# A hybrid encoder trunk on one core: threads for the operands of w_in, new build-time costs and yields, and a sixth group of columns in the woven stage

## The chip, the core and the metric

The kernel runs on one core of one Trainium2 chip. The metric is the device time of one execution in microseconds, the median over several runs. The core has a matrix engine (TensorE, PE in the profile, with its weight loads listed as PEld), a vector engine (VectorE, DVE), a scalar engine (ScalarE, ACT), GpSimd (POOL), and SyncE (SP), whose queue issues all of this kernel's DMAs. Each engine executes its own instructions in the order in which they stand in its queue and waits on semaphores for the others.

## The reference

Two inputs of 512 tokens and 1024 channels (0 and 1 here) go through two layers with shared weights. Everything is float32.

```
layer 0 (RWKV-7):  xn = rms_norm(x, pre0);  r, k, v, z = lerp_j(xn) @ w_r, w_k, w_v;  xn @ w_z
   two scans, forward and backward, per head of 64 channels:
   S_t = S_{t-1} (diag(decay_t) + a_t b_t^T) + v_t k_t^T ;   y_t = S_t r_t
   y = group_norm(y_fwd + y_bwd) + bonus;   h = (y * silu(z)) @ w_o
   x1 = x + rms_norm(h, post0)
layer 1 (2-D neighbourhood attention, 16 heads, window 8 x 16):
   q, k, v, z = rms_norm(x1, pre1) @ w_in + b_in          # w_in: 1024 x 4096
   o = softmax(q k^T / 8 + bias) v;   y = x1 + rms_norm((o * silu(z)) @ w_o + b_o, post1)
```

## The kernel before

Activations lie with channels on partitions, so one tile is 128 channels by 512 tokens, and an operand of a projection is eight such tiles. To keep float32 accuracy, every operand and every weight is split into a rounded part `hi` and a rest `lo` (one ScalarE copy and one VectorE subtraction each), and a product is a triplet of matmuls, hi*hi, hi*lo and lo*hi. A column is 128 output channels: eight triplets into one PSUM bank. One weight column of 128 x 1024 is loaded and split in two halves of 128 x 512.

The program has three stages.

The prelude makes the norms and the mixed inputs and the columns of z and k of input 0.

The woven stage holds the scan. The scan runs in chunks of 64 tokens: 64 steps (8 chunks for each of 4 groups of head pairs and 2 inputs, both directions at once). For each group of 8 steps, `prep` (two per group) makes the decayed vectors and Gram matrices, and `inverse` inverts 32 x 32 triangular blocks by elimination on VectorE (30 times a multiplication L941 and an addition L942), transposes, and joins the blocks on PE (L970, L972). `step` runs the chain PE (L1106, L1112), ScalarE, PE (L1133), ScalarE, PE (L1153, L1157), VectorE (L1163 to L1173) to the next state. `finish` normalises a group's result. Beside this run the projections in `flow`: `loads` and `splits` of weights, `fetched` and `operands` of the tile operands, `products` (L751 to L753) and `posts`, which evict a column. They go through a fixed list of groups: r, v of input 0; k, r, v and six columns of z of input 1; w_o of input 0; two columns of z; and last the columns of w_in for input 0, made in order of p, four columns (q, k, v, z) for each p. `NPA` says for how many p this happens here. Products of w_in need operands that are made from h, the result of w_o: x1 = h * post0 * rstd + x (L1526, L1529), a scaled hi and lo (L728, L733), and the sum of squares (L1534, L1538) for the second norm, whose factor is applied at the eviction (`qkvz`, L1331). Before, one thread does all of this for one tile after the other.

The order in the woven stage is decided when the program is built. Each of these parts is a Python generator, a `Thread`, which yields the engine on which it goes on, a gate, and a function for the time at which its inputs are there. `weave` keeps a `Clock` with a time for each engine, and picks the thread of lowest rank among those whose time has come; PE work comes last, and products have rank 9, so they are what fills PE. What stands between two yields of a thread is issued in one piece. The clock's costs and latencies (`LAT`, and the lines in `one`) are only the planner's: on the chip every engine follows its queue and its waits. `NACT` operand buffers, `NXR` buffers for loaded tiles, and `NW` for split weights bound how far ahead the threads go.

In the third stage the framework's scheduler sets the order. `rest` makes the columns of w_in for the remaining p, then w_o of input 1, with attention for input 0 spread beside them: `run` advances the attention generator by `POST0` for each triplet of w_in and by `POST` for each one of w_o. A head pair has two half-heads there (scores L1375, transposes L1393, output L1408). Then come the second layer's end for input 0, and w_in, attention and w_o of input 1.

Of the kernel before, what the change touches and what calls it, by code (L numbers as in the profile page):

```python
# [19 lines left out]
P = 128  # L20
# [30 lines left out]
class Clock:  # L51
# [4 lines left out]
    LAT = dict(P=200.0, A=45.0, D=45.0, G=90.0, S=0.0)  # L56
# [55 lines left out]
    def one(self, e, i):  # L112
# [102 lines left out]
class Trunk:  # L215
    NACT, NW, NRAW, NXR, NTMP, WP = 18, 4, 3, 3, 5, 512
    POST0, POST, POST2, POST3, NPA = 0.7, 1.0, 0.15, 0.66, 5
# [18 lines left out]
    NZ1, STOCK, EPS, NEAR = 6, 1, 60.0, 400.0  # L236
    AHEADE = dict(S=3000.0, A=200.0, D=200.0)
# [16 lines left out]
    def name(self, s):  # L254
        self.uid += 1
        return f"{s}_{self.uid}"
# [424 lines left out]
    def flow(self):  # L681
# [4 lines left out]
        name = lambda *xs: [x.tensor.name for x in xs]  # L686
        raw, w, x, todo = {}, {}, {}, {}
# [21 lines left out]
        def fetched():  # L709
            for g, (ready, source, _) in enumerate(self.groups):  # L710
                for k in range(KT if g else 0):
                    yield "S", lambda: ready() and 8 * g + k < min(did["x"] + self.NACT // 2 + self.NXR - 1, 8 * len(self.groups) - 8 + did["x1"] + self.NXR)
                    todo[g, k] = source(k)

        def operands():
            for g in range(1, len(self.groups)):
                for k in range(KT):
                    yield "S", lambda: (g, k) in todo
                    src, before, by, then = todo.pop((g, k))
                    for e, f in before:  # L720
                        yield e, None, lambda c: c.at(name(src))
                        f()
                    yield "A", lambda: 8 * g + k < did["x"] + self.NACT // 2 - (by is not None), lambda c: c.at(name(src))
                    lo, hi = self.pair()
                    if by is None:
                        nc.scalar.copy(hi, src)
                    else:
                        nc.scalar.activation(hi, src, AF.Identity, scale=by)  # L728
                    yield "D"
                    if by is None:  # L730
                        nc.vector.tensor_tensor(lo, src, hi.bitcast(F32), op=ALU.subtract)  # L731
                    else:
                        nc.vector.scalar_tensor_tensor(lo, src, by, hi.bitcast(F32), op0=ALU.mult, op1=ALU.subtract)  # L733
                    x[g, k] = hi, lo
                    for e, f in then:
                        yield e
                        f()
# [1117 lines left out]
```

## Time and profile before

| | us |
|---|---|
| median of 3 runs | 1693.5 (1692.28 to 1696.38) |
| profiled execution, its own time | 1695.69 |
| span of that execution | 1693.9 |
| PE busy | 1542.3 |
| DVE busy | 1243.6 |
| ACT busy | 987.9 |
| mean granted clock of PE | 0.958 |

The busy times are unions of the instructions' times within the span. A matmul's listed time overlaps that of the next, so the rate of PE is read from start to start. The costliest lines are the triplets of the woven stage (L751 to L753, 608 of each) and of the third stage (L406 to L408).

### The profile page before, as it was taken

What the parts mean: (1) busy time and instruction counts of PE and PEld (TensorE: products, weight loads), DVE (VectorE), ACT (ScalarE), POOL (GpSimd) and SP (SyncE); (2) the same over time, 40 slices, a digit from 0 to 9 for tenths busy, and PEclk for the clock granted to TensorE, in tenths of its full rate; (3) what the DMA queues carried; (4) which work ended last, traced back from release to release, by engine and by line L of the source; (5) the groups of instructions that cost most, each with busy time, mean ns of one, the idle gap of its engine ahead of it and who ended that gap; (6) DMA issues with size and microseconds to landing.
All of it is one profiled execution on the core that took longest, in us unless ns stands there. A gap on an engine that the chain in (4) does not pass through costs nothing.

```text
span 1693.9 us, 45876 instructions
## 1 busy us (share of the span) xinstructions
PE 1542.3 (91%) x18624; PEld 1171.7 (69%) x18624; DVE 1243.6 (73%) x2725; ACT 987.9 (58%) x1979; POOL 24.1 (1%) x94
## 2 busy tenths in 40 slices
PE   7989788889998988889978689999999999999998
PEld 6767556666676766666656477777777887777776
DVE  8985679688786886897878988656566686555564
ACT  5443655767665666667576545544567765555562
POOL 0000000000000000000000000000000000000000
PEclk9989989899999999999989799999999999999999
DMA  5435687786686777885667754557555346545553
GB/s 207 162 124 187 201 286 222 209 257 224 196 258 197 233 230 220 273 262 188 210 226 233 225 181 141 158 169 261 177 184 181 113 138 240 188 155 174 168 175 106
DMA packets 240819, 336.23 MB, mean 198 GB/s; under 512 B 53696, under 2 KB 119360, under 8 KB 240608
## 3 DMA queue, kind: packets, MB, share of 16 engines
q1 hardware_dynamic: 240608, 333.31, 61.2%
q8 instruction: 146, 2.39, 0.6%
q14 instruction: 65, 0.53, 0.1%
HBM read 227.71 MB, written 105.51 MB: 197 GB/s over the span
## 4 chain that ended last, share of the span: by engine, by line
PE 59%; DVE 16%; DMA 9%; ACT 9%; issue 5%; SPq 1%; DVEq 0%; ACTq 0%
PE pg L406 6%; PE pg L407 6%; PE pg L408 6%; PE pm L751 5%; PE pm L752 4%; PE pm L753 4%; PE sc L1375 2%; PE pf L1035 2%; PE po L1408 2%; DVE etmp L941 2%; DVE N L942 2%; PE pt L1393 1%; PE zy L1106 1%; DVE wlo L705 1%; PE us L1133 1%
## 5 line engine op out<-in xcount | busy, mean ns | idle before, releaser
L751 PE MATMUL pm<-act,whi 128*128 128x512 f32 x608 | 272.5, 448 | 19.4 <-ACT whi L703 8.9
L753 PE MATMUL pm<-act,wlo 128*128 128x512 f32 x608 | 249.2, 410 | 13.3 <-DVE wlo L705 11.9
L752 PE MATMUL pm<-act,whi 128*128 128x512 f32 x608 | 248.6, 409 | 11.2 <-DVE act L731 8.3
L406 PE MATMUL pg<-act,whi 128*128 128x512 f32 x480 | 199.8, 417 | 0.0
L407 PE MATMUL pg<-act,whi 128*128 128x512 f32 x480 | 190.2, 396 | 0.0
L408 PE MATMUL pg<-act,wlo 128*128 128x512 f32 x480 | 189.8, 396 | 0.0
L355 ACT CAST whi<-raw 128x512 fp32r<-128x512 f32 x156 | 96.4, 619 | 134.8 <-PE pg L407 87.9
L751 PEld LDWEIGHTS pm<-act,whi 128*128 128x128 f32 x608 | 119.2, 196 | 60.5 <-issue 13.3
L753 PEld LDWEIGHTS pm<-act,wlo 128*128 128x128 f32 x608 | 119.3, 196 | 50.0 <-DVE wlo L705 19.4
L356 DVE TENSOR_TENSOR wlo<-raw,whi 128x512 fp32r<-128x512 f32 x156 | 106.7, 686 | 59.8 <-ACT whi L355 49.8
L752 PEld LDWEIGHTS pm<-act,whi 128*128 128x128 f32 x608 | 119.7, 197 | 34.8 <-DVE act L731 11.4
L705 DVE TENSOR_TENSOR wlo<-raw,whi 128x512 fp32r<-128x512 f32 x152 | 103.3, 684 | 46.8 <-ACT whi L703 43.7
L703 ACT CAST whi<-raw 128x512 fp32r<-128x512 f32 x152 | 93.1, 618 | 31.4 <-PE pm L752 13.1
L408 PEld LDWEIGHTS pg<-act,wlo 128*128 128x128 f32 x480 | 90.7, 189 | 19.9 <-issue 0.7
L406 PEld LDWEIGHTS pg<-act,whi 128*128 128x128 f32 x480 | 90.9, 189 | 19.4 <-issue 4.8
L407 PEld LDWEIGHTS pg<-act,whi 128*128 128x128 f32 x480 | 91.0, 190 | 17.2 <-issue 3.0
L942 DVE TENSOR_TENSOR N<-etmp,N 128x30 f32<-128x30 f32 (+14 forms) x240 | 79.7, 332 | 8.2
L941 DVE TENSOR_TENSOR etmp<-N 128x30 f32<-128x30 f32 (+14 forms) x240 | 78.4, 327 | 4.5
L1386 DVE CUSTOM_DVE_ANT_0 sb<-sc,bias 128x256 f32<-128x256 f32 x128 | 50.5, 420 | 39.8 <-PE pt L1393 29.2
L1389 ACT ACTIVATE sb<-sb,mx 128x256 f32<-128x256 f32 x128 | 64.2, 503 | 16.4 <-DVE mx L1388 16.0
L1035 PE MATMUL pf<-cab 64*64 64x128 f32 (+1 forms) x2048 | 69.9, 274 | 3.7 <-issue 3.1
L1145 ACT COPY X<-us 64x256 f32<-64x256 f32 x128 | 46.8, 366 | 33.7 <-PE zy L1013 31.2
(381 smaller groups left out, 3298.3 us busy)
## 6 DMA issues: line engine op xcount, KB each, us to landing
dab<-ab SPq DMA_DIRECT2D x32, 1024.0 KB, 7.3
cab<-dab SPq DMA_DIRECT2D x64, 512.0 KB, 4.3
raw<-in_w_in_dram SPq DMA_DIRECT2D x128, 256.0 KB, 3.4
bias<-in_rpb_dram SPq DMA_DIRECT2D x32, 384.0 KB, 4.1
raw<-in_w_z_dram SPq DMA_DIRECT2D x32, 256.0 KB, 5.3
dz<-tmp SPq DMA_DIRECT2D x32, 256.0 KB, 3.3
raw<-in_w_k_dram SPq DMA_DIRECT2D x32, 256.0 KB, 2.6
dk<-tmp SPq DMA_DIRECT2D x32, 256.0 KB, 3.1
```

The lines of the kernel that those rows point to most:

```text
L355: self.nc.scalar.copy(hi, src)
L356: (eng or self.nc.vector).tensor_tensor(lo, src, hi.bitcast(F32), op=ALU.subtract)
L406: nc.tensor.matmul(ps, hi, x[k][0], start=(k == 0), stop=False)
L407: nc.tensor.matmul(ps, hi, x[k][1], start=False, stop=False)
L408: nc.tensor.matmul(ps, lo, x[k][0], start=False, stop=(k == KT - 1))
L705: nc.vector.tensor_tensor(lo, raw.pop(h), hi.bitcast(F32), op=ALU.subtract)
L751: nc.tensor.matmul(ps, hi[:, at], xh, start=(k == 0), stop=False)
L752: nc.tensor.matmul(ps, hi[:, at], xl, start=False, stop=False)
L753: nc.tensor.matmul(ps, lo[:, at], xh, start=False, stop=(k == KT - 1))
L941: vt.tensor_tensor(tv, N[:, q + 1:, q:q + 1].broadcast_to([P, n, q]), N[:, q:q + 1, :q].broadcast_to([P, n, q]), op=ALU.mult)
L942: vt.tensor_tensor(N[:, q + 1:, :q], tv, N[:, q + 1:, :q], op=ALU.add)
L1035: end = nc.tensor.matmul(st.f[half(a), h, 0, d, g] if st.last else st.f[half(a), h, :, d, g], ab[half(h), d, g, 2 * e[d] + 1 - a], rt if s ...
```

## The change

- The planner's clock gets other numbers. A result counts as available later on PE, ScalarE, VectorE and GpSimd (`LAT`), a ScalarE operation costs 85 + 0.85 n in place of 175 + 0.86 n, a VectorE one 82 + 1.02 n in place of 80 + 1.06 n ns, and a ScalarE or VectorE operation that reads its own engine's result is charged the latency too.
- Yields are added between dependent vector operations: in `inverse` between L941 and L942 and in two other places, in `step` between L1165 and L1166, in `prep` and in `finish`, so that the planner may put other work between them.
- The operands of w_in are made by three threads, `residual` (x1), `scaled` (hi and lo) and `squares` (the norm's sum), each of rank 0.6 in place of 2.5. A gate lets five sources be under way; two of the eight (`HACT`, tiles 3 and 4) are loaded into operand buffers in place of the three `xr` buffers, and `held` counts the operand buffers in use.
- `NPA` goes from 5 to 6: the columns of w_in for six p are in the woven stage, 80 columns in place of 76, and for two in the third stage in place of three. `POST0` goes from 0.7 to 0.9.

```diff
-    LAT = dict(P=200.0, A=45.0, D=45.0, G=90.0, S=0.0)
+    LAT = dict(P=210.0, A=125.0, D=116.0, G=120.0, S=0.0)
...
-                    if f != e or e == "S":
+                    if f != e or e == "S" or e in "AD" and table is self.made:
...
-                c = 175.0 + 0.86 * n
+                c = 85.0 + 0.85 * n
...
-                c = 80.0 + 1.06 * n
+                c = 82.0 + 1.02 * n
...
-    POST0, POST, POST2, POST3, NPA = 0.7, 1.0, 0.15, 0.66, 5
+    POST0, POST, POST2, POST3, NPA = 0.9, 1.0, 0.15, 0.66, 6
...
+    HACT = (3, 4)
...
-                    yield "S", lambda: ready() and 8 * g + k < min(did["x"] + self.NACT // 2 + self.NXR - 1, 8 * len(self.groups) - 8 + did["x1"] + self.NXR)
+                    if g < len(self.groups) - 1:
+                        yield "S", lambda: ready() and 8 * g + k < did["x"] + self.NACT // 2 + self.NXR - 1
+                    else:
+                        yield "S", lambda: ready() and k < did["x1"] + 5 and held() + (k in self.HACT) + (k % 3 > 0) <= self.NACT
...
+        def residual():
+            for k in range(KT):
+                yield "S", lambda: (last, k) in todo
+                h, xc = todo[last, k]
+                yield "D", None, lambda c: c.at(name(h))
+                nc.vector.scalar_tensor_tensor(h, h, self.vec("post0", k), self.h_acc, op0=ALU.mult, op1=ALU.mult)
+                yield "D", None, lambda c: c.at(name(h, xc))
+                nc.vector.tensor_tensor(h, h, xc, op=ALU.add)
+                self.save("x1", 0, k, h)
...
+        def scaled():
...
+                yield "A", lambda: held() + 2 <= self.NACT, lambda c: c.at(name(h))
...
+                nc.scalar.activation(hi, h, AF.Identity, scale=self.vec("pre1", k))
+                yield "D"
+                nc.vector.scalar_tensor_tensor(lo, h, self.vec("pre1", k), hi.bitcast(F32), op0=ALU.mult, op1=ALU.subtract)
...
+        def squares():
...
+                nc.scalar.activation(sq, h, AF.Square)
...
+                    nc.vector.tensor_tensor(self.x1_acc, sq, self.x1_acc, op=ALU.add)
...
+            Thread(lambda: 0.6, residual()), Thread(lambda: 0.6, scaled()), Thread(lambda: 0.6, squares()),
...
             vt.tensor_tensor(tv, N[:, q + 1:, q:q + 1].broadcast_to([P, n, q]), N[:, q:q + 1, :q].broadcast_to([P, n, q]), op=ALU.mult)
+            yield "D"
             vt.tensor_tensor(N[:, q + 1:, :q], tv, N[:, q + 1:, :q], op=ALU.add)
...
                 vt.tensor_tensor(st.S, so, before.S, op=ALU.add)
+                yield "D"
                 vt.tensor_tensor(st.S, st.S, wc, op=ALU.mult)
```

More of the change, by code (lines that the diff above doesn't have):

```diff
@@ L713, in fetched, with held @@
                     todo[g, k] = source(k)
+        def held():
+            return 2 * (8 + did["pair"] - did["x"]) + did["act"]
         def operands():
-            for g in range(1, len(self.groups)):
+            for g in range(1, len(self.groups) - 1):
                 for k in range(KT):
                     yield "S", lambda: (g, k) in todo
[L719 to L723, printed above, removed]
+                    src = todo.pop((g, k))
+                    yield "A", lambda: 8 * g + k < did["x"] + self.NACT // 2, lambda c: c.at(name(src))
```

62 lines of the change are left out of this document (33 added, 29 removed).

## The prediction

> **What bounds the kernel now.** I read the page first, for the share of each engine and the granted clock. TensorE (PE) is busy 91% of the span and its clock line has dips only in the first two thirds.
>
> ```profile
> span 1693.9 us, 45876 instructions
> PE 1542.3 (91%) x18624; PEld 1171.7 (69%) x18624; DVE 1243.6 (73%) x2725; ACT 987.9 (58%) x1979; POOL 24.1 (1%) x94
> PEclk9989989899999999999989799999999999999999
> ```
>
> Next I cut the span at the places that the change touches, with the view of busy time by window. Columns: window, its length, busy time (and count) of PE, its weight loads, VectorE (DVE), ScalarE (ACT), GpSimd; then the granted clock, the DMA share, GB/s.
>
> ```profile
> 172.00:836.00 664.00, 581.77 (x10010) 430.61 (x10010) 530.67 (x1018) 427.38 (x847) 16.03 (x39) 0.95 0.73 230
> 836.00:901.00 65.00, 55.13 (x653) 40.46 (x654) 50.43 (x78) 47.26 (x80) 2.11 (x4) 0.84 0.66 220
> 901.00:947.00 46.00, 36.01 (x1164) 28.60 (x1160) 40.62 (x83) 27.74 (x62) 0.23 (x2) 1.00 0.80 252
> 947.00:1028.00 81.00, 68.70 (x704) 50.58 (x702) 68.40 (x127) 45.38 (x77) 2.01 (x3) 0.83 0.56 178
> 1028.00:1134.00 106.00, 100.56 (x2470) 75.85 (x2464) 71.40 (x152) 48.46 (x101) 1.89 (x2) 0.97 0.52 165
> 1134.00:1173.00 39.00, 38.27 (x184) 30.32 (x184) 24.32 (x49) 17.99 (x31) 0.00 (x0) 1.00 0.67 230
> 1173.00:1343.00 170.00, 170.00 (x1042) 132.81 (x1040) 110.16 (x391) 112.14 (x260) 0.00 (x0) 1.00 0.53 174
> 1343.00:1400.00 57.00, 56.92 (x282) 47.45 (x280) 41.36 (x76) 33.55 (x60) 0.00 (x0) 1.00 0.41 128
> 1400.00:1694.00 294.00, 280.55 (x1520) 218.85 (x1520) 165.96 (x497) 146.34 (x328) 0.00 (x0) 0.98 0.53 172
> ```
>
> From 1134 us on, PE is the bound: it is idle for about 14 us in 560, at full clock. In the scan stage, 172 to 1134 us, nothing is the bound for long: PE idles 82.2 + 9.9 + 10.0 + 12.3 + 5.4 = 120 us, and the clock share missing, 664 x 0.05 + 65 x 0.16 + 81 x 0.17 + 106 x 0.03, is at most another 61 us. DVE is busy 79% there. So 181 us of slack on PE, all of it in the stage whose order the change rewrites, is all there is to win; no matrix work is removed.
>
> The last scan step's matmuls, and where the weave's products end, come from the timeline of PE:
>
> ```profile
> 1133.99 0.72 PE L1157 MATMUL zy<-X,R 128*64 128x64 f32 x16
> 1156.82 0.39 PE L751 MATMUL pm<-act,whi 128*128 128x512 f32 x1
> 1157.50 0.39 PE L751 MATMUL pm<-act,whi 128*128 128x512 f32 x1
> 1172.84 0.39 PE L753 MATMUL pm<-act,wlo 128*128 128x512 f32 x1
> ```
>
> The second and third row are the first matmuls of two successive product triplets (L751, L752, L753): 0.68 us a triplet at full clock. The products that are left when the scan has ended run for 39 us with nothing else to hide.
>
> **The change part by part.** *More products inside the scan.* I counted triplets in the built order of both programs on PE's queue. Up to row 657 the two orders agree, so the prelude costs nothing either way. Before, 559 of 608 triplets stand ahead of the last step's L1157; after, 625 of 640, since the sixth group of w_in adds 32. So 66 triplets move from behind the last step to ahead of it: 34 of the weave's own tail, and the 32 of the four columns that leave the stage after it. Behind the last step PE works at full clock without idling, so this takes 66 x 0.683 = 45 us off the tail.
>
> *What those 66 cost ahead of it.* Between 0 (they fit into the 120 us of idle time) and 45 us (PE simply works longer). By steps: before, the counts at steps 40, 48, 56 and 64 are 406, 453, 536, 559; after, 417, 482, 579, 625. So 55 of the 66 fall behind step 40, that is behind 836 us, and need 37.5 us. The rows from 836 to 1134 us have 37.6 us idle and at most 27 us of missing clock. The clearest hole is 901 to 947 us: steps 41 to 48, in which the order before holds 7 triplets and the order after 27. Why it was empty:
>
> ```profile
> L1526 DVE SCALAR_TENSOR_TENSOR xr<-xr,cv,acc x8: 739/744/746, 886.1 to 959.4; 128x512 f32<-128x512 f32 x8
> ```
>
> The eight operands of w_in are made one after the other over 73 us, for 0.744 us of this step each. The three threads put the DVE work of all eight into 53 rows of its order instead of 131. I take 15 us, a third of 45: the hole is real, but a queue in order never fills idle time without delaying the scan somewhat.
>
> *The yields and the charge for a result of its own engine.*
>
> ```profile
> 940.12 0.42 DVE L1165 TENSOR_TENSOR S<-us,S 128x256 f32<-128x256 f32 x1 [0.31 <-issue]
> 940.58 0.42 DVE L1166 TENSOR_TENSOR S<-S,wc 128x256 f32<-128x256 f32 x1
> 940.92 0.41 DVE L1173 TENSOR_TENSOR y<-zy,y 128x256 f32<-128x256 f32 x1
> 941.85 0.68 DVE L1538 TENSOR_TENSOR vs<-tmp,vs 128x512 f32<-128x512 f32 x1
> 942.46 0.74 DVE L1526 SCALAR_TENSOR_TENSOR xr<-xr,cv,acc 128x512 f32<-128x512 f32 x1
> 943.84 0.36 DVE L941 TENSOR_TENSOR etmp<-N 128x198 f32<-128x198 f32 x1
> 944.24 0.37 DVE L942 TENSOR_TENSOR N<-etmp,N 128x198 f32<-128x198 f32 x1
> ```
>
> L1166 reads L1165's result and starts 0.46 us after it; L1173 reads nothing of L1166, has the same size and starts 0.34 us after it. A result read at once costs 0.12 us more; the two elimination rows, 0.40 us apart at 198 elements, are such a pair too. Before, 368 of the elimination's successive pairs (L941, L942) stand directly one behind the other, after, 207; of the state updates 48 and 6. 203 gaps of 0.12 us are 24 us of DVE time at most, nothing at least. DVE sets the pace only in the handovers between two groups of steps (836 to 901 and 947 to 1028 us are two of them), about half of the stage, so I take 12 us.
>
> [...]
>
> *Fewer stalls on operands.* The waits of PE in the scan stage, longest in total first (us, times, longest):
>
> ```profile
> PE pm L753 <- DVE wlo L705: 11.9, 14, 4.2
> PE pm L751 <- ACT whi L703: 8.9, 5, 5.4
> PE pm L752 <- DVE act L731: 8.3, 5, 4.0
> PE pm L751 <- ACT act L728: 4.0, 1, 4.0
> PE zy L1112 <- DVE N L942: 4.0, 1, 4.0
> ```
>
> The first four are products that the build-time clock placed before their operands were there: 33 us. The clock before charges a dependent pair on one engine no delay, so for 480 elimination operations it is up to 480 x 0.12 = 58 us ahead of DVE over the stage, and PE waits for DVE at places the planner thought safe. The new clock charges that. A stall costs twice, as the timeline after the one at 951 us shows:
>
> ```profile
> 966.34 0.63 PE L751 MATMUL pm<-act,whi 128*128 128x512 f32 x1
> 967.62 0.63 PE L751 MATMUL pm<-act,whi 128*128 128x512 f32 x1
> ```
>
> Here a triplet takes 1.28 us in place of 0.68. Bounds: 0, and 33 us of waits with as much again of clock. Part of that room is already used for the 66 triplets, so I take 12 us.
>
> [...]
>
> *The stage behind.* Attention for input 0 has 16 half-heads. Before, they spread over the 20 columns from 1173 to 1343 us; after, the first four columns in the built order run without attention and the 16 share twelve columns. DVE was busy 110.2 of 170 us, ACT 112.1. Attention there takes about 170 - 20 x 8 x 0.683 = 61 us of PE (some columns reach past the window, so this is a lower bound), and twelve columns another 66: 127 us, in which DVE still has at least 110.2 less the eight columns' conversions and evictions, about 8 x 3 x 0.61 = 15 (two splits and an eviction a column, at the 0.61 us from L1538 to L1526): 95 of 127, 75%. PE stays the bound, with little room for one late chain: +5 us, between 0 and 15. The tail of the kernel is as before.
>
> The sum, against the profiled execution's own 1695.7 us: -45 + 15 - 12 - 12 + 5 = -49, so 1647. That execution is 2.2 us above the median of the runs, 1693.5, which gives **1644 us**. With the ends of each term that go together (half of them good, half bad) it lies between about 1615 and 1675.
>
> **The rivals.**
>
> *The elimination is torn apart (slower).* The handover from one group of steps to the next waits for the inverse, a chain of 60 vector operations. With a yield between every two, 161 more of its links in the order have other work between them. A 128x512 operation takes 0.61 us from start to start (L1538 to L1526 above), less the 0.12 saved: 0.49 us a break, 79 us in all if each lies on the chain. Against the forecast that is 1644 + 79 = 1723; it decides when more than 100 of the 161 breaks delay a handover. For it: the steps of a group do wait, and the planner gives elimination a low rank. Against it: the work between has to be done anyway, and DVE is idle for a fifth of the stage.
>
> *The products only move.* The scan is bound by PE after all: the 66 triplets cost their full 45 us, nothing else changes, and the stage behind is 5 us longer: 1693.5 + 5 = 1698. For it: windows in which PE is busy over 93%. Against it: 120 us idle. Here belongs also that the new orders do not hold on the chip as planned.
>
> [...]
>
> *The whole slack shrinks.* The 66 triplets are free, DVE gains its 24, and stalls return 33 with the stage behind at +5: 1693.5 - 45 - 24 - 33 + 5 = 1597. For it: the clock dips after stalls, so one avoided stall returns more than itself. Against it: DVE at 79% leaves some handovers as they are.
>
> **How the numbers follow.** Forecast 0.50; nothing from the spread chain 0.13; whole slack 0.15; products only move 0.07; elimination torn apart 0.15. What a measurement can tell from no change is about 0.3%, 5 us. So faster 0.78, same 0.07, slower 0.15. The range of 1595 to 1700 takes in all but the slower rival and a little below the best one.
>
> **What would show it.** Right: the last L1157 (its counterpart) between 1095 and 1140 us with a third or more of the 120 us idle gone, no hole in steps 41 to 48, the clock from 836 to 1028 us above 0.9; the eight operands made in about 40 us; attention's stage without idle PE. Wrong: a last step at 1160 us or later; handovers of over 65 us with DVE running other work between the links; a new stall where a loaded source waits for its buffer on SP's queue with the weights behind it.

## The result, and the profile after

| | us |
|---|---|
| before, median of 20 runs | 1694.68 (1687.25 to 1701.81) |
| after, median of 20 runs | 1699.09 (1695.16 to 1705.33) |
| ratio | 1.0028, 95% interval 1.0015 to 1.0041 |
| profiled execution of after, its own time | 1703.37 |

The change made the kernel about 4 us slower, where 49 us less were forecast. The page of the changed kernel, the same three lines as before: PE has the same 18624 matmuls and is busy 11 us longer, and the clock line has five dips as before, but deeper ones, down to 5 where the lowest was 7.

```profile
span 1701.6 us, 45922 instructions
PE 1553.2 (91%) x18624; PEld 1183.1 (70%) x18624; DVE 1228.3 (72%) x2725; ACT 983.7 (58%) x1979; POOL 24.1 (1%) x94
PEclk9989999999999997997985999999999999999999
```

The timeline of PE in the changed kernel shows where the last step is (L1196 is the old L1157) and where the weave's products end (L788 is the old L753):

```profile
1179.24 0.70 PE L1196 MATMUL zy<-X,R 128*64 128x64 f32 x16
1196.35 0.40 PE L788 MATMUL pm<-act,wlo 128*128 128x512 f32 x1
```

The scan ends at 1179 us in place of 1134, and the products 17.5 us behind it in place of 39.2. What is left behind them is 504.8 us in place of 520.7. So the tail became 21.7 + 15.9 = 37.6 us shorter, and the scan 45.2 us longer: +7.7 us in the two profiled executions.

The scan as one window, before:

```profile
172.00:1134.00 962.00, 842.17 (x14978) 626.10 (x14978) 761.53 (x1453) 596.22 (x1166) 22.27 (x50) 0.94 0.69 219
```

and after:

```profile
172.00:1179.00 1007.00, 896.05 (x15173) 670.27 (x15171) 763.37 (x1480) 609.50 (x1190) 22.27 (x50) 0.92 0.68 215
```

PE is busy 53.9 us longer, VectorE 1.8, ScalarE 13.3. PE's idle time is 1007 - 896 = 111 us against 120: most of the time that the prediction meant to fill is still there. Cut at the first and last matmuls of the steps, the eight stretches of steps take 417.1 us (412.4 before), and the eight stretches ahead of them, in which the next group's inverse is made, 590.1 us (549.6). So 40 of the 45 us lie in the handovers. The third stage, by contrast, did what was forecast, but for one stall of PE on an operand of w_o, in the timeline at 1356 us:

```profile
1356.45 1.22 PE L407 MATMUL pg<-act,whi 128*128 128x512 f32 x2 [6.68 <-ACT act L356]
```

One handover, from 853 to 931 us, can be read step by step. The eight operands of w_in are made here, now in 43 us, as the rows of the first (L741, x1) and the last (L757, lo) of their operations on VectorE tell by the starts of the first and last instruction:

```profile
L741 DVE SCALAR_TENSOR_TENSOR xr<-xr,cv,acc x6: 741/747/748, 886.5 to 925.7; 128x512 f32<-128x512 f32 x6
L757 DVE SCALAR_TENSOR_TENSOR act<-xr,cv,act x6: 743/752/753, 888.8 to 928.9; 128x512 fp32r<-128x512 f32 x6
```

The windows of this handover and of the steps behind it show a granted clock of 0.72 in the handover and 0.97 in the steps:

```profile
853.00:931.00 78.00, 58.95 (x650) 43.53 (x650) 66.68 (x112) 48.45 (x86) 2.11 (x4) 0.72 0.74 238
931.00:989.00 58.00, 53.09 (x1229) 40.92 (x1225) 46.44 (x103) 34.37 (x72) 0.24 (x2) 0.97 0.63 200
```

The timelines of VectorE, ScalarE and PE in it, each row with the wait ahead of it in brackets:

```profile
905.50 0.69 DVE L1262 TENSOR_TENSOR bv<-pm,bv 128x512 f32<-128x512 f32 x1 [4.08 <-DMA bv<-dv]
907.75 1.96 DVE L988 STREAM_TRANSPOSE NA<-N 128x1024 f32<-128x1024 f32 x1
910.20 1.94 DVE L993 STREAM_TRANSPOSE MT<-N 128x1024 f32<-128x1024 f32 x1
909.76 1.92 PE L1009 MATMUL pm<-NA,Go 32*32 32x32 f32 x64 [7.17 <-DVE NA L988]
912.17 2.11 ACT L997 COPY MT<-MT 32x1024 f32<-32x1024 f32 x2 [13.68 <-DVE MT L993]
915.08 0.80 PE L786 MATMUL pm<-act,whi 128*128 128x512 f32 x1 [3.40 <-ACT act L755]
```

VectorE waits 4.1 us for a reloaded v at the head of its queue. Behind it stand the two transposes that end the elimination. PE waits for the first, ScalarE for the second, and behind ScalarE's wait stand the operands of w_in, on which PE waits once more. The granted clock is halved from 896.8 us for 34.1 us, so from before this wait, which begins at 901.4. So a wait of 4.1 us on one queue is followed by 7.2 + 3.4 us of PE waiting on two others, in a handover that is 12.7 us longer than its counterpart before (64.9 us). That the wait makes the handover longer is not shown. The kernel before has a wait of nearly the same length on the same reload in the counterpart, as its timeline of VectorE tells:

```profile
879.43 0.69 DVE L1221 TENSOR_TENSOR bv<-pm,bv 128x512 f32<-128x512 f32 x1 [3.86 <-DMA bv<-dv]
```

The last pair of experiments tried to take the wait away.

### The profile page after: what moved, and what is told of

Read it like the earlier page. It is cut to its first block, busy times and chain, and to the rows that moved or that the text cites. A ratio compares the mean times of both kernels' runs of the same rounds, so it can differ in the third digit from the quotient of the medians.

```text
span 1701.6 us, 45922 instructions
## 1 busy us (share of the span) xinstructions
PE 1553.2 (91%) x18624; PEld 1183.1 (70%) x18624; DVE 1228.3 (72%) x2725; ACT 983.7 (58%) x1979; POOL 24.1 (1%) x94
## 4 chain that ended last, share of the span: by engine, by line
PE 46%; DVE 3%; ACT 2%; DMA 2%; issue 1%; DVEq 0%; ACTq 0%; SPq 0%
PE pg L407 6%; PE pg L408 6%; PE pg L409 6%; PE pm L786 4%; PE pm L787 3%; PE pm L788 3%; PE sc L1416 2%; PE po L1449 2%; PE pt L1434 2%; PE pf L1074 1%; PE us L1192 1%; PE us L1172 1%; PE zy L1145 1%; PE pm L1403 1%; PE zy L1196 1%
## 5 line engine op out<-in xcount | busy, mean ns | idle before, releaser
L786 PE MATMUL pm<-act,whi 128*128 128x512 f32 x640 | 291.8, 456 | 29.8 <-ACT act L731 10.0
L787 PE MATMUL pm<-act,whi 128*128 128x512 f32 x640 | 264.3, 413 | 13.6 <-DVE act L733 13.2
L788 PE MATMUL pm<-act,wlo 128*128 128x512 f32 x640 | 262.1, 410 | 6.7 <-DVE wlo L707 6.7
L407 PE MATMUL pg<-act,whi 128*128 128x512 f32 x448 | 183.3, 410 | 6.7 <-ACT act L356 6.7
L786 PEld LDWEIGHTS pm<-act,whi 128*128 128x128 f32 x640 | 125.7, 196 | 79.7 <-issue 15.5
L408 PE MATMUL pg<-act,whi 128*128 128x512 f32 x448 | 179.8, 401 | 0.7 <-DVE act L357 0.7
L409 PE MATMUL pg<-act,wlo 128*128 128x512 f32 x448 | 178.4, 398 | 0.0
L787 PEld LDWEIGHTS pm<-act,whi 128*128 128x128 f32 x640 | 127.1, 199 | 40.3 <-DVE act L733 19.0
L788 PEld LDWEIGHTS pm<-act,wlo 128*128 128x128 f32 x640 | 126.9, 198 | 37.1 <-DVE wlo L707 9.0
L707 DVE TENSOR_TENSOR wlo<-raw,whi 128x512 fp32r<-128x512 f32 x160 | 109.1, 686 | 41.5 <-ACT whi L705 41.4
L407 PEld LDWEIGHTS pg<-act,whi 128*128 128x128 f32 x448 | 85.5, 191 | 26.1 <-ACT act L356 6.9
L408 PEld LDWEIGHTS pg<-act,whi 128*128 128x128 f32 x448 | 85.7, 191 | 18.8 <-issue 2.6
L409 PEld LDWEIGHTS pg<-act,wlo 128*128 128x128 f32 x448 | 85.4, 191 | 18.2 <-issue 0.9
L1097 DVE TENSOR_TENSOR AK<-zy,cc 128x256 f32<-128x256 f32 x63 | 26.7, 423 | 58.5 <-PE zy L1052 58.5
```

Of the source, the lines that this page charges most:

```text
L407: nc.tensor.matmul(ps, hi, x[k][0], start=(k == 0), stop=False)
L408: nc.tensor.matmul(ps, hi, x[k][1], start=False, stop=False)
L409: nc.tensor.matmul(ps, lo, x[k][0], start=False, stop=(k == KT - 1))
L707: nc.vector.tensor_tensor(lo, raw.pop(h), hi.bitcast(F32), op=ALU.subtract)
L786: nc.tensor.matmul(ps, hi[:, at], xh, start=(k == 0), stop=False)
L787: nc.tensor.matmul(ps, hi[:, at], xl, start=False, stop=False)
```

## The experiments

"Last step" is the start of the last step's last matmul group in its profile, 1134.0 us before and 1179.2 after. Ratios are to the kernel before on the same chip, with the 95% interval. The kernels in which one cost is cut have the time of one run each, beside 1694 to 1696 us of the kernel before.

**The parts, each alone.** The four parts of the change, each put into the kernel before.

only_clock: the planner's numbers.

```diff
-    LAT = dict(P=200.0, A=45.0, D=45.0, G=90.0, S=0.0)
+    LAT = dict(P=210.0, A=125.0, D=116.0, G=120.0, S=0.0)
-                    if f != e or e == "S":
+                    if f != e or e == "S" or e in "AD" and table is self.made:
-                c = 175.0 + 0.86 * n
+                c = 85.0 + 0.85 * n
-                c = 80.0 + 1.06 * n
+                c = 82.0 + 1.02 * n
```

> The kernel before with the new costs and latencies of the planner's clock alone. In its order 607 of 608 product triplets stand ahead of the last scan step (before: 559). Theory A (the scan's time is the PE work in its queue plus stalls that do not shrink when products are put among them): the scan grows by 48 x 0.68 = 33 us, the tail shrinks by as much, the time is within 8 us of before. Theory B (the calibrated clock does win, and another part of the change takes it back): 20 to 45 us faster than before.

only_threads: the three threads, `HACT`, the gates of the loads.

```diff
+    HACT = (3, 4)
...
+        def residual():
...
+        def scaled():
...
+        def squares():
```

> The kernel before with the three threads for the operands of w_in alone. 587 of 608 triplets ahead of the last step, the additional 28 nearly all from step 41 on. Theory A: within 8 us of before. Theory B in the form that the threads of rank 0.6 push the inverse back on the vector engine: 10 to 30 us slower than before, with the handover after step 40 longer than its 65 us. Were the starved stretch at 901 to 947 us really lost time, as the prediction took it: 15 to 25 us faster.

only_yields: the yields.

```diff
             vt.tensor_tensor(tv, ...)
+            yield "D"
             vt.tensor_tensor(N[:, q + 1:, :q], tv, N[:, q + 1:, :q], op=ALU.add)
```

> The kernel before with the added yields alone. 587 of 608 triplets ahead of the last step. Theory A: within 8 us of before, less at most 12 us for the vector engine's distances of 0.12 us. The rival of the prediction (the elimination is torn apart): 20 us slower or more, with longer handovers. With the yields a win by themselves: 10 to 15 us faster.

only_six: the sixth group of columns, and the spread of attention.

```diff
-    POST0, POST, POST2, POST3, NPA = 0.7, 1.0, 0.15, 0.66, 5
+    POST0, POST, POST2, POST3, NPA = 0.9, 1.0, 0.15, 0.66, 6
```

> The kernel before with six groups of columns in the woven stage and attention spread at 0.9 alone. The order up to the last step is that of before (559 triplets), 81 triplets follow it in place of 49, and the third stage has 32 fewer. All theories: the scan ends at 1134 us as before; the sum of the tail and the third stage is the same but for attention, which shares twelve columns in place of twenty: 0 to 10 us slower.

| | time us | ratio | last step | weave ends | products ahead of last step |
|---|---|---|---|---|---|
| only_clock | 1710.45 | 1.0097 (1.0078 to 1.0115) | 1187.5 | 1189.0 | 607 of 608 |
| only_threads | 1677.93 | 0.9894 (0.9860 to 0.9929) | 1138.5 | 1160.6 | 587 of 608 |
| only_yields | 1687.71 | 0.9967 (0.9950 to 0.9983) | 1149.8 | 1171.8 | 587 of 608 |
| only_six | 1700.68 | 1.0048 (1.0030 to 1.0066) | 1130.1 | 1192.4 | 559 of 640 |

In microseconds: +17, -15, -6, +7, sum +3, close to the whole change's +4. The +17 is what neither theory had. The new clock alone makes the last step late by 53 us. With 607 products ahead of it, nearly none is left behind, yet the weave ends 16 us later than before. The threads do what they were meant to: the windows of only_threads show the scan 4 us longer with 28 more products in it, and the weave's rest 22 us long in place of 39.

```profile
172.00:1138.00 966.00, 862.25 (x15057) 642.58 (x15056) 768.63 (x1464) 601.60 (x1175) 22.26 (x50) 0.94 0.69 220
1138.00:1161.00 23.00, 23.00 (x115) 18.07 (x114) 13.01 (x20) 8.89 (x15) 0.00 (x0) 1.00 0.49 157
```

The gain of 15 us is the one written down for the case that the starved stretch of steps 41 to 48 was lost time. But only 4 of the 28 products fall into that stretch (11 in place of 7, 48.0 us in place of 45.7), and 25 into the handover behind it, which goes from 81.4 to 89.0 us: about 0.3 us for each.

The sixth group alone does not make the scan longer (1130.1 us); its third stage is 12 us shorter, its weave 19 us longer, and PE's idle time in the third stage goes from 13.4 to 21.0 us.

**Do the parts add?**

threads_yields: both of the parts that gained.

```diff
+        def residual():
...
+            yield "D"
             vt.tensor_tensor(N[:, q + 1:, :q], tv, N[:, q + 1:, :q], op=ALU.add)
```

> The kernel before with the three threads and the yields, without the new clock and without the sixth group. If the parts add up as the single runs suggest (threads 0.9894, yields 0.9967): 0.986 of before, 1671 us, the fastest so far. If they win the same time twice: 1678 us, like the threads alone.

clock_cost and clock_lat: the two halves of the clock, costs of an operation, and latencies with the charge for a result of the own engine.

```diff
-                c = 175.0 + 0.86 * n
+                c = 85.0 + 0.85 * n
-                c = 80.0 + 1.06 * n
+                c = 82.0 + 1.02 * n
```

> The kernel before with only the planner's new costs of an operation (ScalarE 85 + 0.85 n in place of 175 + 0.86 n, VectorE 82 + 1.02 n), the old latencies. 504 triplets ahead of the last step in its order (before 559). Theory C (the cheaper ScalarE operation is what hurts: the planner believes the engine free and places work that PE then waits for): 10 us slower or more, PE idle in the scan above 140 us. Theory D (the latencies are what hurts, by products put into the handovers in place of short waits): within 8 us of before, the scan shorter by the 55 triplets, 38 us.

```diff
-    LAT = dict(P=200.0, A=45.0, D=45.0, G=90.0, S=0.0)
+    LAT = dict(P=210.0, A=125.0, D=116.0, G=120.0, S=0.0)
-                    if f != e or e == "S":
+                    if f != e or e == "S" or e in "AD" and table is self.made:
```

> The kernel before with only the planner's new latencies and the charge for a result of the same engine, the old costs. All 608 triplets stand ahead of the last step. Theory C: within 8 us of before. Theory D: 15 to 30 us slower, the handovers longer by 40 us or more and the steps as before.

no_clock and no_six: the changed kernel without the clock's numbers, and without the sixth group and the spread.

```diff
-    LAT = dict(P=210.0, A=125.0, D=116.0, G=120.0, S=0.0)
+    LAT = dict(P=200.0, A=45.0, D=45.0, G=90.0, S=0.0)
...
-                c = 85.0 + 0.85 * n
+                c = 175.0 + 0.86 * n
...
```

> The changed kernel with the planner's old clock: threads, yields and the sixth group. 592 triplets ahead of the last step, 620 other operations in the eliminations. If the parts simply add (clock 1.0097, six 1.0048, threads with yields 0.9992): 1.004 of before, 1701 us, and the new clock cost nothing here beyond that. If the clock's 17 us come on top in the changed kernel: 1683 us.

```diff
-    POST0, POST, POST2, POST3, NPA = 0.9, 1.0, 0.15, 0.66, 6
+    POST0, POST, POST2, POST3, NPA = 0.7, 1.0, 0.15, 0.66, 5
```

> The changed kernel with five groups and attention at 0.7. The order up to the last handover is that of the changed kernel; all 608 triplets stand ahead of the last step. If the sixth group costs 7 us here as it does alone: 1692 us. If it pays because the scan would else run out of products: 1705 us or more.

| | time us | ratio | last step |
|---|---|---|---|
| threads_yields | 1692.29 | 0.9992 (0.9971 to 1.0013) | 1160.1 |
| clock_cost | 1724.51 | 1.0178 (1.0156 to 1.0201) | 1128.0 |
| clock_lat | 1713.96 | 1.0105 (1.0070 to 1.0139) | 1191.4 |
| no_clock | 1715.13 | 1.0114 (1.0072 to 1.0156) | 1163.0 |
| no_six | 1706.06 | 1.0065 (1.0037 to 1.0093) | 1185.4 |

They do not add. Threads and yields gain 15 and 6 alone and 1 together. Each half of the clock costs more alone (30 and 18) than both (17). The clock costs 17 in the kernel before and gains 16 in the changed one (1715.13 against 1699.09). The sixth group costs 7 in the kernel before, 23 beside threads and yields with the old clock (no_clock against threads_yields), and gains 7 with the new one (no_six against after). (These last three compare medians of different series; by the ratios to the kernel before they are 15, 21 and 6 us.) Of what was written down for threads_yields and no_clock neither outcome came; no_six came out as written for a scan that runs out of products: its last product ends at 1151.6 us and the scan goes on to 1185.4. That the sum of the parts alone comes near the whole is chance.

One pattern runs through these kernels. With the new latencies and the inverse's rank as it was, the last step lies between 1179 and 1191 us (after, only_clock, clock_lat, no_six, and after_need below); with the old ones between 1128 and 1163 us (before and seven others). clock_lat alone puts it 57.4 us later, with 49 more products ahead of it. The handovers take 51.8 us of that (601.4 in place of 549.6), as was written down for theory D. clock_cost takes 55 products out of the scan, which becomes 6.0 us shorter, and puts them behind it, where the weave takes 78.5 us in place of 39.2: theory C has the size of the loss, but PE's idle time in the scan is 133 us and not above 140. The five late kernels also share a wait of VectorE for a product of PE, 50 to 59 us in place of 25 to 37, of which the traces of before and after show:

```profile
DVE AK L1058 <- PE zy L1013: 25.0, 23, 3.6
DVE AK L1097 <- PE zy L1052: 58.5, 53, 3.5
```

That this wait makes the scan late is not shown: in dve_lite, below, it is 55.7 us and the last step is early. What makes two of these orders differ by 15 us stays open.

**What paces the scan?** Five kernels keep the order of the kernel before, since the planner is told the old sizes, and cut the cost of one resource in the woven stage, the fifth of three at once. They leave out work that the result needs, and serve for timing alone.

pe_lite: the third matmul of each triplet covers 64 of its 512 columns.

```diff
-                    nc.tensor.matmul(ps, lo[:, at], xh, start=False, stop=(k == KT - 1))
+                    nc.tensor.matmul(ps[:, :64], lo[:, at], xh[:, :64], start=False, stop=(k == KT - 1))
```

> The order of before in the woven stage, but the third matmul of each triplet (L753) runs over 64 of its 512 columns, with the planner charged for all (the rest of that product is left out). 558 such matmuls lie ahead of the last step; each may save up to 0.19 us, 106 us in all. If the scan is paced by vector and scalar engine and PE's products only fill its idle time, the last step moves little, by less than 25 us, and PE's idle time in the scan grows by what is saved. If PE work is on the path in full (theory A), the last step comes 80 us earlier or more and the idle time stays near 120 us.

dve_lite: each elimination operation covers one column of its q.

```diff
-            vt.tensor_tensor(N[:, q + 1:, :q], tv, N[:, q + 1:, :q], op=ALU.add)
+            one = vt.tensor_tensor(N[:, q + 1:, :1], tv[:, :, :1], N[:, q + 1:, :1], op=ALU.add)
```

> The order of before in the woven stage, with the elimination's 480 operations narrowed to one column (most of the elimination's arithmetic is left out), the planner charged for the full width. Each operation falls from 0.33 us to about 0.1 to 0.2 us: 60 to 100 us of vector time, 8 to 12 us an inverse. Theory E: the last step comes earlier by 50 us or more, although PE's order and work in the scan are those of before. Were PE the pace, or the DMA: less than 15 us.

split_lite: both operations of a weight's split cover 128 of 512 columns, and the products use these 128 for every k.

```diff
-                nc.scalar.copy(hi, raw[h])
+                one = nc.scalar.copy(hi[:, :P], raw[h][:, :P])
...
-                nc.vector.tensor_tensor(lo, raw.pop(h), hi.bitcast(F32), op=ALU.subtract)
+                one = nc.vector.tensor_tensor(lo[:, :P], raw.pop(h)[:, :P], hi[:, :P].bitcast(F32), op=ALU.subtract)
...
-                    at = slice(k % 4 * P, k % 4 * P + P)
+                    at = slice(0, P)
```

> The order of before in the woven stage, with the split of a weight half over 128 of its 512 columns on ScalarE and VectorE, the planner charged for all (the products use these 128 columns for every k, so they are not the reference's). 0.33 us of ScalarE and 0.39 us of VectorE less for each of some 140 splits ahead of the last step: 46 and 55 us. Theory G (the products' vector and scalar work paces the scan): the last step 30 us earlier or more. Theory H (the scan is paced by its own chain and order): less than 12 us.

dma_lite: a quarter of each weight is loaded, and the split repeats it four times, so that ScalarE and VectorE work as long as before.

```diff
+                    one = nc.sync.dma_start(raw[2 * c + j][:, :P], src[:, j * self.WP:j * self.WP + P])
```

> The order of before, with a quarter of each weight half loaded in the woven stage and the split spread over the whole by repeating it (so the products are not the reference's): three quarters of 40 MB less to move. Theory I (loads of weights hold up the splits, and through ScalarE's queue the scan): the last step 20 us earlier or more, the waits of the splits for their loads gone. Theories G and H: less than 10 us.

all_lite: pe_lite, split_lite and dma_lite together (the elimination as it was). after_all_lite: the same three edits in the changed kernel, in the changed kernel's order.

```diff
+                    one = nc.sync.dma_start(raw[2 * c + j][:, :P], src[:, j * self.WP:j * self.WP + P])
...
+                one = nc.scalar.copy(hi[:, :P], raw[h][:, :P])
...
+                    nc.tensor.matmul(ps[:, :64], lo[:, at], xh[:, :64], start=False, stop=(k == KT - 1))
```

> The order of before with all three at once: the third matmul of a triplet over 64 columns, splits over 128, loads of a quarter. Theory G: the last step 50 us earlier or more, at 1085 us or below. Theory H: still 1110 us or later, as what is left is the scan's own chain.

> The order of the changed kernel with all three at once. If the 45 us between 1134 and 1179 us come from what the additional products need (their matmuls, splits and loads), the last step falls to within 12 us of that of the same cut in the order of before. If they come from the order in which the planner put the scan's own operations, it stays 30 us or more behind it.

The windows of the scan, in turn pe_lite, dve_lite, split_lite, dma_lite, all_lite, after_all_lite (columns: window, length, busy time and count of PE, its weight loads, VectorE, ScalarE, GpSimd, clock, DMA share, GB/s):

```profile
172.00:1135.00 963.00, 793.13 (x14975) 623.17 (x14973) 760.55 (x1452) 595.20 (x1164) 22.31 (x50) 0.90 0.69 218
```

```profile
172.00:1123.00 951.00, 840.35 (x14977) 629.26 (x14977) 698.52 (x1453) 597.26 (x1166) 22.27 (x50) 0.94 0.70 221
```

```profile
172.00:1121.00 949.00, 843.35 (x14974) 632.12 (x14973) 707.29 (x1451) 550.67 (x1163) 22.27 (x50) 0.93 0.70 221
```

```profile
172.00:1123.00 951.00, 839.67 (x14972) 626.43 (x14970) 761.52 (x1451) 595.30 (x1165) 22.40 (x50) 0.94 0.62 191
```

```profile
172.00:1101.00 929.00, 785.12 (x14978) 622.68 (x14976) 705.20 (x1451) 549.53 (x1165) 22.32 (x50) 0.91 0.64 196
```

```profile
172.00:1121.00 949.00, 819.96 (x15165) 653.75 (x15163) 697.77 (x1477) 558.22 (x1188) 22.31 (x50) 0.90 0.64 195
```

| | time of one run, us | last step | against 1134.0 |
|---|---|---|---|
| pe_lite | 1690.45 | 1134.8 | +0.8 |
| dve_lite | 1681.29 | 1123.4 | -10.6 |
| split_lite | 1682.77 | 1121.4 | -12.6 |
| dma_lite | 1684.62 | 1123.1 | -10.9 |
| all_lite | 1656.86 | 1100.7 | -33.3 |
| after_all_lite | 1640.40 | 1121.0 | -13.0 (1179.2 after: -58.2) |

pe_lite is the plainest. PE is busy 49 us less, 0.09 us for each of the 558 matmuls where up to 0.19 was written down, and the scan is as long as it was: idle time goes from 120 to 170 us, and the missing clock, by the windows, from 962 x 0.06 = 58 to 963 x 0.10 = 96 us. So the PE work cut does not set the pace of the scan. It is not a pure cut: the lower clock makes the rest of PE's work slower (at half clock a triplet took 1.28 us in place of 0.68, in the prediction's timeline), and what the cut would give at an unchanged clock is not shown. In this stage 49 us less work on the busiest engine by the windows, PE at 88%, give nothing, and 63 us less on the second, VectorE at 79%, give 10.6 us. VectorE, the splits and the loads are each worth a little, between 10 and 13 us, none sets the pace alone, and the products' costs together are worth 33 us, more than the 23 us of splits and loads apart. split_lite, dma_lite and all_lite each lie between the two outcomes written down for them. No pure form of a theory, one engine, the elimination or the loads, survives this.

The pair of all_lite and after_all_lite splits the 45 us. With the products made cheap, the changed kernel's last step is still 1121.0 - 1100.7 = 20.3 us later: at most that much lies in the order of the scan's own operations, since a cheap product still has two full matmuls, its operands and its eviction. The other 24.9 us go with the cost of the products; how much of it is PE's in this order was not run apart. This lies between the two outcomes written down for it, and neither theory gets all. The changed order is better then as a whole, by 16.5 us (1640.40 against 1656.86): its tail is shorter, and the scan pays less for it. These are single runs.

**Is it the elimination's place?** after_rank: in the changed kernel the elimination gets a rank ahead of `prep`, the plain operands and the splits of weights.

```diff
-            ... Thread(lambda: 5, inverse()), ...
+            ... Thread(lambda: 1.4, inverse()), ...
```

> The changed kernel with the inverse at rank 1.4 in place of 5, so that the planner prefers the elimination's next operation to weight splits, plain operands and preps. In its order 323 other vector operations stand inside the eliminations of groups 1 to 7 (changed kernel 675, kernel before 606), and 540 triplets ahead of the last step (625). Theory E (the scan's length is the eliminations', and these are as long as the other vector work put into them): eliminations 2 to 7 shorter by 30 us or so each, the last step 60 us earlier or more than the changed kernel's 1179 us; the time falls by the part that the 85 triplets behind it, 58 us, do not take back: 0 to 30 us faster than the changed kernel. Theory A (PE): the last step earlier by just the 85 triplets, the time the same within 8 us.

1748.97 us, 1.0313 (1.0293 to 1.0333). The mechanism of the rival is there: before, after and in after_rank, the last matmul group of a group's first step starts within 10 us of the end of its inverse. Within the last seven eliminations, from the first transpose to the start of the transpose that ends it, 661 VectorE operations of other threads (423 us) stand after, 592 (375 us) before. after_rank brings them to 39 to 50 for each group, and one link directly follows the other in the timeline of VectorE:

```profile
719.85 0.38 DVE L980 TENSOR_TENSOR N<-etmp,N 128x220 f32<-128x220 f32 x1
720.26 0.38 DVE L978 TENSOR_TENSOR etmp<-N 128x210 f32<-128x210 f32 x1
720.67 0.38 DVE L980 TENSOR_TENSOR N<-etmp,N 128x210 f32<-128x210 f32 x1
```

The eliminations become 50 to 60 us long in place of 50 to 109, the handovers 521.0 us in place of 590.1, and the steps 469.6 in place of 417.1. Of the vector work that was kept out of the elimination only little comes back between the steps, where VectorE is busy 332.6 us in place of 320.3; what makes the steps 52 us longer stays open. The last step is 16.4 us earlier, at 1162.8, with 540 of 640 products ahead of it in place of 625, and the kernel ends 50 us later: neither outcome written down came. Here it did not pay to keep the elimination whole.

**A wait at the head of a queue.** after_need and threads_need: the changed kernel, and only_threads, with a readiness for the reloaded v in `finish`.

```diff
-            yield "D"
+            yield "D", None, need(bv)
             vt.tensor_tensor(bv, bp, bv, op=ALU.mult)
```

> The changed kernel with one readiness added: in finish, the yield ahead of the multiplication into bv now waits, in the planner, for the time at which the reloaded v has landed; nothing else is edited. In the trace of the changed kernel VectorE waits 12.7 us in 4 places for that reload, with the elimination's transposes queued behind one of them: the 4.1 us wait that ends at 905.5 us is followed by 13.7 us of ScalarE waiting for the inverse, by 7.2 and 3.4 us of PE waiting and by 34.1 us at half clock. Theory of waits at the head of a queue: such chains are what the scan is longer by, so the last step (1179 us) comes 12.7 to 30 us earlier, 1149 to 1167, and the kernel takes 1669 to 1687 us. Theory of the order as a whole (many small delays, none of which decides): the wait goes but others appear, the last step lies within 10 us of 1179 and the kernel within 0.5% of 1699 us.

> The kernel before with the three threads for the operands of w_in alone (1677.9 us, 0.9894 of before), and the same one readiness added in finish. There VectorE waits 14.1 us for the reload, in 4 places, the longest 6.5 us. Theory of waits at the head of a queue: the last step (1138.5 us) comes 14 us or more earlier and the kernel takes 1664 us or less, 0.981 of before. Theory of the order as a whole: within 7 us of 1678, 0.985 to 0.9935 of before, in either direction.

after_need takes 1717.39 us, 1.0123 (1.0079 to 1.0167), last step 1180.7; threads_need 1679.63 us, 0.9913 (0.9883 to 0.9943), last step 1140.8. The wait was not taken away. The waits of VectorE in after_need:

```profile
DVE bv L1262 <- DMA bv<-dv: 15.6, 4, 5.7
```

It was 12.7 us in 4 places, and it is 20.8 in threads_need, where it was 14.1: the planner takes the reload for landed before it is. So these two do not decide whether such waits make the scan longer. The other traces speak against it: the kernel before waits for this reload as long as the changed one, 13.4 us in 4 places, and only_clock, whose last step is at 1187.5 us, only 2.9 us.

```profile
DVE bv L1221 <- DMA bv<-dv: 13.4, 4, 5.4
```

The two runs show something else: one readiness, which removes no work and no wait, moves the changed kernel by 18 us and the other by 2.

The fastest version is only_threads, 0.9894 (0.9860 to 0.9929) of before; it beats both kernels.

## Why the prediction was wrong, point by point

**The tail: right.** 45 us less and 5 more for the denser attention were forecast, 40 together; 37.6 were measured. The 625 of 640 products ahead of the last step are as counted, the third stage is 15.9 us shorter, and the short chain that was feared for it shows as the stall of 6.7 us at 1356.

**What the 66 cost ahead of the last step: this step failed.** The sum had +15 for it, between 0 and 45, and with -12 and -12 the scan was to end 9 us earlier; it ended 45.2 us later, and these 54 us are the whole error but for the 2.4 of the tail. The failed thought is the opening one, that PE's idle time and missing clock are what there is to win. pe_lite gave the scan 50 us more of idle time and the last step did not move: what the scan waits for lies elsewhere, and PE's idle time does not tell what more work there will cost. A product that moves into the scan brings its loads, its splits on ScalarE and VectorE and its eviction with it and stands in four queues ahead of the scan's own operations. The term was costed on PE alone, by triplets of 0.68 us. With its third matmul, its loads and its splits made cheap, 24.9 of the 45 us go, where the sum had 15 for the whole; the 20.3 us that stay are a term that the sum did not have, the order of the scan's own operations, and the two gains of 12 us do not show in the scan. That makes 10 + 20 + 24 = 54, if the parts are taken to add. The hole that the prediction named, steps 41 to 48, was filled as said (27 triplets in place of 7), and that stretch grew from 45.7 to 58.2 us, 12.5 us for 20 triplets, 0.63 us each, nearly the 0.68 of a triplet on PE. But there is no one price. 28 more products ahead of the last step came with 4.5 us more in only_threads and 15.8 in only_yields, 48 with 53.5 in only_clock; 55 fewer with 6.0 less in clock_cost. The 0.23 us a product that the sum used lies within these. The order decides, and what in the order does is not shown.

**The spread vector chain: mis-sized.** Taken as 12 us, half of 24. dve_lite returned 10.6 us for 63 us of VectorE's time, a sixth; at that share 24 us would be worth 4, an estimate. The yields alone gained 6 us in all. The distance of 0.12 us that the term started from is not in doubt, and the pairs of dve_lite in the last section show one as well; what was mis-sized is how much of VectorE's time is on the path. The kernel's time cannot tell a gain of 0, to which the prediction gave a chance of 0.13, from one of 12 us: either is lost among the differences between orders. In the trace of dve_lite an independent operation starts 0.11 us after one that takes 0.20 us, a dependent one 0.23 us after one that takes 0.19.

**Fewer stalls on operands: failed.** 12 us were taken for the new latencies and the charge; there are not fewer, and alone (clock_lat) they make the kernel 18 us slower. The waits of PE in the scan, after:

```profile
PE pm L787 <- DVE act L733: 13.2, 12, 2.7
PE pm L786 <- ACT act L731: 10.0, 7, 2.5
PE pm L786 <- ACT whi L705: 9.6, 3, 5.3
PE pm L1009 <- DVE NA L988: 7.6, 2, 7.2
PE pm L788 <- DVE wlo L707: 6.7, 4, 3.3
PE pm L786 <- ACT act L755: 6.7, 2, 3.4
```

Waits on operands and weights are 13.2 + 10.0 + 9.6 + 6.7 + 6.7 = 46 us, where 33 were quoted before. The largest moved from the weights' lo parts (L753 before, 11.9 us) to the lo and hi parts of the projections' operands (L733 and L731), most of them at 242 to 252, 543 to 548 and 755 to 782 us. The clock missing in the scan, by the windows, went from 962 x 0.06 = 58 to 1007 x 0.08 = 81 us. That a stall costs as much again in clock, the upper bound of the term, was the author's estimate. The triplets of 1.28 us behind the stall of 4.0 us at 951 us do not show it: in the kernel before the clock was halved from 948.6 us for 20.5 us, with PE busy for 2.75 of the 5 us ahead of it, and that stall begins at 951.3. Of the signs set down as right, the eight operands in about 40 us (43) and the filled hole came true; the clock above 0.9 in that stretch (0.72) and a third of PE's idle time gone (111 us of 120 are left) did not; a last step at 1160 us or later was set down as wrong, and it is 1179.

**The rivals.** "The products only move" named 1698 us and the full 45 us for the 66 products. The numbers are close to those measured (1699 and 45.2), but by luck: its reason, that PE bounds the scan, is the one that pe_lite speaks against, and part of the 45 us does not go with the products at all. "Torn apart" has its mechanism in the trace and not its price (after_rank). The chances were set on the size of PE's idle time, a number that did not tell which order gains, and hence 0.78 for faster was far too sure. Fourteen orders of nearly the same work lie between 1678 and 1749 us; a sum of local terms of 5 to 15 us could not tell two of them apart.

## What to carry to other kernels

Here PE's 120 us of idle time in the scan told neither what could be won nor what more work there would cost: cut the engine's work with the order held, and see whether the end moves, before a forecast is built on it. Price work that is moved on every engine and queue that serves it, not on the one where it is largest. Constants of a planner, better ones too, are part of a set with its ranks and gates: measure every combination that is to be kept, since here gains of 15 and 6 us gave 1 together, and the one part that gained most was best alone. Where the order of queues decides, a forecast from local terms deserves a wide range.

## What the runs showed of the hardware

Less work for PE came with a lower clock: in pe_lite the granted clock of the scan went from 0.94 to 0.90 while PE was busy 49 us less. The longest half-clock stretch after, 34.1 us from 896.8, holds the end of a wait of PE of 3.3 us, up to 898.0, and the waits of 7.2 and 3.4 us; the rest of it lies where PE was at work, with these waits in between up to 915 us and hardly any idle time behind. The window of it, and of its last 16 us:

```profile
897.00:931.00 34.00, 22.41 (x359) 16.13 (x361) 25.19 (x38) 15.91 (x26) 1.89 (x2) 0.50 0.66 211
915.00:931.00 16.00, 15.92 (x286) 12.00 (x288) 12.46 (x19) 11.89 (x22) 0.29 (x1) 0.50 0.47 158
```

PE is busy for 22.4 of the 34 us, and for 15.9 of the last 16, and stays at half clock.

The narrow vector operations of dve_lite took about 0.19 us each. dve_lite's elimination cut 320 to 330 ns operations to one column, at most 30 elements, and they took, by line, count, total and mean ns:

```profile
L945 DVE TENSOR_TENSOR N<-etmp,N 128x30 f32<-128x30 f32 (+14 forms) x240 | 45.5, 190 | 8.2
L943 DVE TENSOR_TENSOR etmp<-N 128x30 f32<-128x30 f32 (+14 forms) x240 | 43.9, 183 | 4.5
```

Two dependent ones start 0.23 to 0.24 us apart in its timeline, and an independent one follows sooner: 0.23 us from L943 to L945, 0.11 from there to L707.

```profile
252.36 0.19 DVE L943 TENSOR_TENSOR etmp<-N 128x23 f32<-128x23 f32 x1
252.59 0.20 DVE L945 TENSOR_TENSOR N<-etmp,N 128x23 f32<-128x23 f32 x1
252.70 0.69 DVE L707 TENSOR_TENSOR wlo<-raw,whi 128x512 fp32r<-128x512 f32 x1
253.30 0.20 DVE L943 TENSOR_TENSOR etmp<-N 128x22 f32<-128x22 f32 x1
253.54 0.20 DVE L945 TENSOR_TENSOR N<-etmp,N 128x22 f32<-128x22 f32 x1
253.78 0.20 DVE L943 TENSOR_TENSOR etmp<-N 128x21 f32<-128x21 f32 x1
```
